# MLA's keys made with the features on the partitions, the rotated key turned once

## The chip, the cores and the metric

The kernel runs on one core of a Trainium2 chip (trn2). The metric is the device time of one execution in microseconds. The chip's engines are called here as the profile calls them: PE (TensorE, with PEld its weight loads), ACT (ScalarE), DVE (VectorE), POOL (GpSimd) and SP (SyncE).

## The reference, cut to what matters

One layer of a decoder: two attentions in parallel from one input projection, their gates, a cross-attention and an MLP, for 512 tokens of width 2048 in float32. The change concerns MLA, the second attention: 16 heads, each key of 64 features made from a normed latent of 256, and 32 rotated features that all heads share.

```python
c_q, c_kv, k_r = ...                       # columns of xn @ w_in: 512, 256, 32
q = (rmsnorm(c_q, g_q) @ w_uq).reshape(b, s, 16, 64 + 32)
q_rope = apply_rope(q[..., 64:], cos, sin)
ckv = rmsnorm(c_kv, g_kv)
k_nope = (ckv @ w_uk).reshape(b, s, 16, 64)
v = (ckv @ w_uv).reshape(b, s, 16, 64)
k_r = apply_rope(k_rope, cos, sin)         # one for all heads
sc = (q_nope . k_nope + q_rope . k_r) * 96 ** -0.5
o = softmax(causal(sc)) @ v
```

## The kernel before, in words

Every float32 operand is split into a high part (rounded by a copy on ACT) and a low part (the rest, by a subtraction on DVE); `split` does this and `mm` issues three matmuls per product: high by high, high by low, low by high. Weights come by DMA into raw tiles and are split too.

The program is one stream per engine, and its order comes from how the Python code is run. The main stream is a row of projections. `chunk` makes a projection with tokens on the partitions: for each of four token tiles `tt` it adds up the products in one PSUM tile of up to 512 columns and calls `evac`. `ft` makes a tile of one of the 32 gates (48 matmuls of 128x512), and `gate` ends it: DVE multiplies by `rbc`, ACT takes tanh, a DMA issued on ACT stores it. Between the products of a projection or gate `Side.run` lets steps of a second stream in: the attention, item by item (`attend`: scores and softmax of one item merged with the values of the item before; `flush`: the values of the last item with nothing merged), and the `post` generator of the last projection, which does the transposes. `end_post` runs the rest of a `post` at once, `drain` the rest of the post and of the attention.

PSUM has eight banks: four for `mm` tiles, three for `st` (scores and transposes) and one for the attention's output.

The MLA part: `proj_m` makes the query latent (512), the key latent (256) and the 32 features to rotate in two chunks; its `post` takes the sums of squares on ACT, rotates on POOL, then transposes the latents (three groups of four) and last works out the two roots `rq` and `rkv` in `rsqrt` (a square root on ACT, five steps on DVE). The norm's scale is thus applied later: `mla_q` and `mla_kv` evacuate with `scale=`. There are four quarters of four heads. For each `mla` runs `mla_q` (query projection, rotation, `heads_T`), some gates, `mla_kv`, some gates and a drain, while the quarter before is attended to. `mla_kv` makes 512 columns, keys of four heads and values of four heads, for one token tile at a time; the keys go with the shared rotated part, which POOL copies to each head, into rows of 96 per head, and `heads_T` turns these, four transposes a head and 16 groups of four in all. The last item of the first attention (NSA) has its values merged with the first MLA head's scores.

Of the kernel before, what the change touches and what calls it, by code (L numbers as in the profile page):

```python
# [10 lines left out]
F32R = mybir.dt.float32r  # L11
AF = mybir.ActivationFunctionType
OP = mybir.AluOpType
# [268 lines left out]
class Side:  # L282
# [20 lines left out]
            self.post = None  # L303

    def end_post(self):
        while self.post is not None:
            self.starved = False
            self.step_post()
            if self.starved and not self.step():
                raise RuntimeError("no area is free")  # L310

    def run(self, n, post):
        if post and self.post is not None:
# [17 lines left out]
class Layer:  # L331
# [619 lines left out]
    def proj_m(self, rate):  # L951
        nc = self.nc
        self.ssq = self.cp.tile([128, 8], F32, name="ssq")
        self.ssk = self.cp.tile([128, 4], F32, name="ssk")
        self.cq, self.ckv, self.cpairs = [], [], []

        def evac(c):
            def f(tt, ps):
                nc.scalar.activation(self.Rv(tt, NC_M[c]), ps, AF.Copy, scale=self.rx[:, tt:tt + 1])
            return f  # L960

        def post(c):
            for tt in range(4):
                r = self.Rv(tt, 512)
                sq = self.gst
                n = 384 if c == 0 else 128
                nc.scalar.activation(sq[:, :n], r[:, :n], AF.Square, accum_out=self.ssq[:, 4 * c + tt:4 * c + tt + 1])
                if c:
                    nc.scalar.activation(sq[:, 128:384], r[:, 128:384], AF.Square, accum_out=self.ssk[:, tt:tt + 1])
                    self.rope(r[:, 384:416].rearrange("p (n d) -> p n d", n=1), 1, 0, ROT_B, C_CB, C_SB, tt)  # L970
                    nc.gpsimd.tensor_copy(r[:, 416:448], r[:, 384:416])
            yield
            for j in range(3):
                ps = self.new_st()
                for tt in range(4):
                    nc.tensor.transpose(ps[:, tt * 128:tt * 128 + 128], self.Rv(tt, 512)[:, j * 128:j * 128 + 128],
                                        self.ident)
                f = c * 3 + j
                if f % 2 == 0:
                    self.cpairs.append(self.pairs.get())  # L980
                t, o = self.cpairs[-1], 1024 * (f % 2)
                h = HL(t[:, o:o + 512], t[:, o + 512:o + 1024])
                self.split(h, ps, self.gains[:, G_Q + f:G_Q + f + 1])
                (self.cq if f < 4 else self.ckv).append(h)
                yield
            if c:
                nc.vector.tensor_add(self.ssq[:, :4], self.ssq[:, :4], self.ssq[:, 4:])
                self.rq = self.rsqrt(self.ssq[:, :4], 4, 512, "rq")
                self.rkv = self.rsqrt(self.ssk, 4, 256, "rkv")

        for c in range(2):
            self.chunk("M", c, NC_M[c], evac(c), rate)
            self.side.post = post(c)
# [23 lines left out]
        return out  # L1017

    def mla_kv(self, q, rate):
        nc = self.nc  # L1020
        out = []
        vs = self.pairs.get()
        vv = vs[:, :2048].rearrange("p (h k d) -> p h k d", h=4, k=4)

        def evac(tt, ps):
            sc = self.rkv[:, tt:tt + 1]
            r = self.Rv(tt, 384).rearrange("p (n d) -> p n d", n=4)
            p = ps.rearrange("p (w n d) -> p w n d", w=2, n=4)
            nc.scalar.activation(r[:, :, :64], p[:, 0], AF.Copy, scale=sc)
            nc.gpsimd.tensor_copy(r[:, :, 64:], self.Rv(tt, 512)[:, None, 416:448].to_broadcast([128, 4, 32]))  # L1030
            hi, lo = vv[:, :, tt, :64], vv[:, :, tt, 64:]
            nc.scalar.activation(hi.bitcast(F32R), p[:, 1], AF.Copy, scale=sc)
            nc.vector.scalar_tensor_tensor(lo.bitcast(F32R), p[:, 1], sc, hi, op0=OP.mult, op1=OP.subtract)

        self.chunk("ukv", q, 512, evac, rate, nk=2, xs=self.ckv)
        self.side.post = self.heads_T(4, out.append)
        return out, vs

    def mla_items(self, q, qs, ks, vs):
# [10 lines left out]
    def mla(self, rate):  # L1050
        gates = deque(range(2 * KT))

        def fill(n, r=rate):
            for _ in range(min(n, len(gates))):
                self.gate(gates.popleft(), r)

        fill(T["f0"], T["rf"])
        qs = self.mla_q(0, T["rf"])
        fill(T["f1"], T["rf"])
        self.side.drain()  # L1060
        ks, vs = self.mla_kv(0, T["rf"])
        fill(T["f2"], T["rf"])
        self.side.drain()
        for q in range(4):
            self.side.add(self.attend(self.mla_items(q, qs, ks, vs)))
            if q == 3:
                break
            qs = self.mla_q(q + 1, rate)
            fill(T["f3"])
            ks, vs = self.mla_kv(q + 1, rate)  # L1070
            fill(T["f4"])
            self.side.drain()
        self.side.end_post()
        self.put(*self.cpairs, *self.R)
        self.N = []
        self.n_load = self.load_o(self.d_nsa, self.N)
        while gates:
            fill(1)
            for _ in range(2):
                if self.slots.free:  # L1080
                    next(self.n_load, None)
        self.side.drain()
        self.put(*self.X)
# [707 lines left out]
```

## Time and profile before

| what | value |
| --- | --- |
| three runs | 2912.94, 2912.91, 2905.77 us; median 2912.91 |
| the profiled execution | 2906.3 us, span 2904.5 us, granted clock 0.997 |
| busy share of the span | PE 98%, PEld 84%, DVE 65%, ACT 51%, POOL 13% |
| DMA | 446.61 MB, mean 154 GB/s |
| MLA part | about 580 to 1110 us of the span |

The span runs from the first to the last instruction; the execution is 1.8 us longer. Busy shares are means over the whole span, in which the stages differ. Rows with a time ahead show an instruction's start and length; "[2.65 <-DVE s L820]" behind a row means that its engine sat idle for 2.65 us and that DVE's instruction of line 820 ended it. Starts on one engine lie closer than the lengths say, since an instruction begins while the one before still drains.

### The profile page before, as it was taken

Reading aid. Unit: us, or ns where it says so; the run is one execution under the profiler, and the core shown is the slowest. Engines: PE = TensorE matmul, PEld = TensorE weight load, DVE = VectorE, ACT = ScalarE, POOL = GpSimd, SP = SyncE. Lnnn points to the kernel's source line nnn. Section 1 sums busy time; section 2 is a strip of 40 time slices with the busy share of each in tenths; the row PEclk is TensorE's granted clock in tenths of the full one; section 3 lists DMA queues with packets and bytes.
Section 4 is the critical chain, followed back from the end, with each engine's and each line's share of the span. In section 5 each row is a group of like instructions: output and inputs, shape, how many; then the busy total and the mean of one; then the engine's idle time right before and its main releaser. Section 6 shows DMA issues by size and latency. Waiting matters only on the chain. (4 is left out here: it accounts for less than half of the span.)

```text
span 2904.5 us, 38739 instructions
## 1 busy us (share of the span) xinstructions
PE 2854.6 (98%) x14276; PEld 2436.6 (84%) x14276; DVE 1884.5 (65%) x3225; ACT 1485.4 (51%) x2676; POOL 384.0 (13%) x637
## 2 busy tenths in 40 slices
PE   8999999999999999999999999999999999999997
PEld 8999999888888888888887778888888888888886
DVE  6346666654555555464445767677766788888887
ACT  6345555554444444333235766666666544444444
POOL 3110210002011001000100111111111111111110
PEclk9999999999999999999999999999999999999999
DMA  5322222223323345543433888888889988888895
GB/s 156 98 80 59 59 60 63 63 80 97 98 97 100 102 129 183 187 155 120 123 98 116 197 197 203 216 211 200 221 224 244 230 217 216 221 219 223 221 228 139
DMA packets 158462, 446.61 MB, mean 154 GB/s; under 512 B 16192, under 2 KB 41152, under 8 KB 158272
## 3 DMA queue, kind: packets, MB, share of 16 engines
q1 hardware_dynamic: 90560, 274.24, 29.0%
q0 software_dynamic: 36864, 134.23, 24.5%
q10 hardware_dynamic: 30848, 35.66, 3.5%
q8 instruction: 112, 1.84, 0.3%
q14 instruction: 78, 0.64, 0.1%
HBM read 406.32 MB, written 37.75 MB: 153 GB/s over the span
## 5 line engine op out<-in xcount | busy, mean ns | idle before, releaser
L371 PE MATMUL mm<-s,s 128*128 128x512 f32 (+5 forms) x2008 | 754.4, 376 | 6.3 <-ACT s L378 5.2
L373 PE MATMUL mm<-s,s 128*128 128x512 f32 (+5 forms) x2008 | 729.9, 364 | 2.8 <-DVE s L382 2.8
L372 PE MATMUL mm<-s,s 128*128 128x512 f32 (+5 forms) x2008 | 728.8, 363 | 0.2 <-DVE s L379 0.2
L379 DVE TENSOR_TENSOR s<-s,s 128x512 fp32r<-128x512 f32 (+4 forms) x558 | 366.5, 676 | 250.6 <-ACT s L378 247.2
L371 PEld LDWEIGHTS mm<-s,s 128*128 128x128 f32 x2008 | 379.8, 189 | 55.6 <-issue 5.5
L373 PEld LDWEIGHTS mm<-s,s 128*128 128x128 f32 x2008 | 378.5, 189 | 52.6 <-DVE s L382 4.8
L372 PEld LDWEIGHTS mm<-s,s 128*128 128x128 f32 x2008 | 380.3, 189 | 41.3 <-DVE s L379 1.0
L1536 PE MATMUL mm<-s,s 128*128 128x512 f32 x1024 | 399.5, 390 | 5.7 <-DVE s L1358 5.7
L1535 PE MATMUL mm<-s,s 128*128 128x512 f32 x1024 | 403.6, 394 | 0.0
L1537 PE MATMUL mm<-s,s 128*128 128x512 f32 x1024 | 399.9, 390 | 0.3 <-DVE s L1431 0.3
L378 ACT CAST s<-s 128x512 fp32r<-128x512 f32 (+4 forms) x558 | 305.5, 570 | 167.2 <-PE mm L372 54.5
L1358 DVE TENSOR_TENSOR s<-d,s 128x1024 fp32r<-128x1024 f32 x202 | 244.9, 1222 | 115.9 <-ACT s L1353 115.8
L1353 ACT CAST s<-d 128x1024 fp32r<-128x1024 f32 x202 | 209.6, 1048 | 194.7 <-DMA d<-wts 176.7
L1535 PE MATMUL st<-s,s 128*128 128x512 f32 x672 | 263.8, 393 | 0.0
L1537 PE MATMUL st<-s,s 128*128 128x512 f32 x672 | 261.9, 390 | 0.0
L1536 PE MATMUL st<-s,s 128*128 128x512 f32 x672 | 261.6, 389 | 0.0
L519 ACT ACTIVATE PP<-PP,mx 128x512 f32<-128x512 f32 (+1 forms) x208 | 116.3, 559 | 274.7 <-DVE mx L518 274.1
L1536 PEld LDWEIGHTS mm<-s,s 128*128 128x128 f32 x1024 | 192.8, 188 | 45.6 <-DVE s L1358 7.0
L1358 DVE TENSOR_TENSOR s<-s,s 128x1024 fp32r<-128x1024 f32 x150 | 181.0, 1221 | 74.8 <-ACT s L1353 74.8
L1537 PEld LDWEIGHTS mm<-s,s 128*128 128x128 f32 x1024 | 192.5, 188 | 41.8 <-DVE s L1431 1.2
L1535 PEld LDWEIGHTS mm<-s,s 128*128 128x128 f32 x1024 | 192.6, 188 | 38.4
L1353 ACT CAST s<-s 128x1024 fp32r<-128x1024 f32 x150 | 153.8, 1048 | 132.0 <-DMA s<-wts 122.9
(308 smaller groups left out, 4152.2 us busy)
## 6 DMA issues: line engine op xcount, KB each, us to landing
s<-wts SPq DMA_DIRECT2D x258, 512.0 KB, 3.7
d<-wts POOLq DMA_DIRECT2D x132, 512.0 KB, 9.8
d<-wts SPq DMA_DIRECT2D x70, 512.0 KB, 7.5
PP<-wts POOLq DMA_DIRECT2D x68, 512.0 KB, 9.5
s<-wts POOLq DMA_DIRECT2D x56, 512.0 KB, 7.3
s<-wts SPq DMA_DIRECT2D x64, 352.0 KB, 3.0
d_u<-s ACTq DMA_DIRECT2D x64, 256.0 KB, 5.6
PP<-wts SPq DMA_DIRECT2D x28, 512.0 KB, 5.4
```

The lines of the kernel that those rows point to most:

```text
L371: t.matmul(ps, a.hr, b.hr, start=first, stop=False)
L372: t.matmul(ps, a.hr, b.lr, start=False, stop=False)
L373: t.matmul(ps, a.lr, b.hr, start=False, stop=last)
L378: nc.scalar.copy(o.hr, src)
L379: nc.vector.tensor_sub(o.lr, src, o.hi)
L519: nc.scalar.activation(p, p, AF.Exp, bias=mx, scale=-1.0, accum_out=sm)
L1353: self.nc.scalar.copy(t.hr, self.raw[i])
L1358: self.nc.vector.tensor_sub(t.lr, r, t.hi)
L1535: m(ps, a.hr, b.hr, start=first, stop=False, skip_group_check=True)
L1536: m(ps, a.hr, b.lr, start=False, stop=False, skip_group_check=True)
L1537: m(ps, a.lr, b.hr, start=False, stop=last, skip_group_check=True)
```

## The change

The key latent is multiplied by its norm's scale in `proj_m` (L979) before it is turned, so that nothing behind it has to scale. `rkv` is therefore worked out ahead of the transposes. The last 96 columns of the latent's row, whose last 32 are the rotated features, are turned in a group of their own (L985) and rows 64 to 96 of the result kept as `self.kr`.

`mla_kv` makes the keys with the features on the partitions: the weights stand still, the latent's 512 tokens move, and two heads of 64 features fill the 128 partitions of one PSUM tile; there are two such tiles in a quarter. ACT copies each head's 64 rows to an SBUF tile (L1049). The values are made as before with tokens on the partitions, 256 columns for each token tile, and two token tiles lie in the two halves of one PSUM tile. ACT writes their high part (L1057), DVE the low one (L1058). A head's key is then split from its 64 rows, and the turned rotated part is copied below it (L1069, L1070); the 16 groups of head transposes for the keys are no longer there. `mla` adds `flush` behind the first `mla_q`, so the last NSA item's values run by themselves and end in the drain ahead of the first `mla_kv`.

Of the changed kernel line numbers above L307 are 3 higher, above `mla_kv` 14 (`mm` has L374 to L376 for L371 to L373, `split` L381 and L382 for L378 and L379, `gate` L1012 to L1014 for L998 to L1000).

```diff
@@ -303,11 +303,14 @@
             self.post = None
 
     def end_post(self):
+        stuck = False
         while self.post is not None:
             self.starved = False
             self.step_post()
             if self.starved and not self.step():
-                raise RuntimeError("no area is free")
+                if stuck:
+                    raise RuntimeError("no area is free")
+                stuck = True
 
     def run(self, n, post):
         if post and self.post is not None:
@@ -968,8 +971,20 @@
                 if c:
                     nc.scalar.activation(sq[:, 128:384], r[:, 128:384], AF.Square, accum_out=self.ssk[:, tt:tt + 1])
                     self.rope(r[:, 384:416].rearrange("p (n d) -> p n d", n=1), 1, 0, ROT_B, C_CB, C_SB, tt)
-                    nc.gpsimd.tensor_copy(r[:, 416:448], r[:, 384:416])
             yield
+            if c:
+                rkv = self.rsqrt(self.ssk, 4, 256, "rkv")
+                for tt in range(4):
+                    r = self.Rv(tt, 512)[:, 128:384]
+                    nc.scalar.activation(r, r, AF.Copy, scale=rkv[:, tt:tt + 1])
+                while not self.slots.free:
+                    self.side.starved = True
+                    yield
+                ps, self.kr = self.new_st(), self.slot_hl(96)
+                for tt in range(4):
+                    nc.tensor.transpose(ps[:96, tt * 128:tt * 128 + 128], self.Rv(tt, 512)[:, 320:416], self.ident)
+                self.split(self.kr[64:], ps[64:96])
+                yield
             for j in range(3):
                 ps = self.new_st()
                 for tt in range(4):
@@ -986,7 +1001,6 @@
             if c:
                 nc.vector.tensor_add(self.ssq[:, :4], self.ssq[:, :4], self.ssq[:, 4:])
                 self.rq = self.rsqrt(self.ssq[:, :4], 4, 512, "rq")
-                self.rkv = self.rsqrt(self.ssk, 4, 256, "rkv")
 
         for c in range(2):
             self.chunk("M", c, NC_M[c], evac(c), rate)
@@ -1017,23 +1031,47 @@
         return out
 
     def mla_kv(self, q, rate):
+
         nc = self.nc
         out = []
         vs = self.pairs.get()
         vv = vs[:, :2048].rearrange("p (h k d) -> p h k d", h=4, k=4)
-
-        def evac(tt, ps):
-            sc = self.rkv[:, tt:tt + 1]
-            r = self.Rv(tt, 384).rearrange("p (n d) -> p n d", n=4)
-            p = ps.rearrange("p (w n d) -> p w n d", w=2, n=4)
-            nc.scalar.activation(r[:, :, :64], p[:, 0], AF.Copy, scale=sc)
-            nc.gpsimd.tensor_copy(r[:, :, 64:], self.Rv(tt, 512)[:, None, 416:448].to_broadcast([128, 4, 32]))
+        w = self.W.get(("ukv", q, 0))
+        ps = [self.new_mm() for _ in range(4)]
+        for i in range(2):
+            for kk in range(2):
+                o = kk * 512 + i * 128
+                self.mm(ps[i], w[:, o:o + 128], self.ckv[kk], kk == 0, kk == 1)
+            self.side.run(rate / 2, True)
+        self.W.mid()
+        self.side.end_post()
+        for j in range(4):
+            nc.scalar.copy(self.Rv(j, 512)[:64], ps[j // 2][64 * (j % 2):64 * (j % 2) + 64])
+        for tt in range(4):
+            p = ps[2 + tt // 2][:, tt % 2 * 256:tt % 2 * 256 + 256]
+            for kk in range(2):
+                self.mm(p, self.ckv[kk][:, tt * 128:tt * 128 + 128], w[:, kk * 512 + 256:kk * 512 + 512],
+                        kk == 0, kk == 1)
+            p = p.rearrange("p (n d) -> p n d", n=4)
             hi, lo = vv[:, :, tt, :64], vv[:, :, tt, 64:]
-            nc.scalar.activation(hi.bitcast(F32R), p[:, 1], AF.Copy, scale=sc)
-            nc.vector.scalar_tensor_tensor(lo.bitcast(F32R), p[:, 1], sc, hi, op0=OP.mult, op1=OP.subtract)
-
-        self.chunk("ukv", q, 512, evac, rate, nk=2, xs=self.ckv)
-        self.side.post = self.heads_T(4, out.append)
+            nc.scalar.copy(hi.bitcast(F32R), p)
+            nc.vector.tensor_sub(lo.bitcast(F32R), p, hi)
+            if tt % 2:
+                self.side.run(rate / 2, True)
+
+        def post():
+            for j in range(4):
+                while not self.slots.free:
+                    self.side.starved = True
+                    yield
+                h = self.slot_hl(96)
+                self.split(h[:64], self.Rv(j, 512)[:64])
+                nc.scalar.copy(h.hr[64:], self.kr.hi[64:])
+                nc.scalar.copy(h.lr[64:], self.kr.lo[64:])
+                out.append(h)
+                yield
+
+        self.side.post = post()
         return out, vs
 
     def mla_items(self, q, qs, ks, vs):
@@ -1056,6 +1094,7 @@
 
         fill(T["f0"], T["rf"])
         qs = self.mla_q(0, T["rf"])
+        self.side.add(self.flush())
         fill(T["f1"], T["rf"])
         self.side.drain()
         ks, vs = self.mla_kv(0, T["rf"])
@@ -1071,7 +1110,7 @@
             fill(T["f4"])
             self.side.drain()
         self.side.end_post()
-        self.put(*self.cpairs, *self.R)
+        self.put(*self.cpairs, *self.R, self.kr)
         self.N = []
         self.n_load = self.load_o(self.d_nsa, self.N)
         while gates:
```

The order of instructions at the places that the prediction speaks of follows; a row is line, operation, out<-in and shape, and what it waits for. The first place is ACT after the squares of `proj_m`'s second post (L522 is the exponential of NSA's softmax, L519 before). Before:

```order
L969 ACTIVATE s_137,ssk<-s_136 128x256 [waits Activation_49]
L519 ACTIVATE PP,sm<-PP,mx 128x512 [waits DVE_49]
L519 ACTIVATE pc,csm<-pc,cmx 128x32 [waits DVE_49]
L381 ACTIVATE d_5916<-st,gains 128x512 [waits PE_49]
L519 ACTIVATE PP,sm<-PP,mx 128x384 [waits DVE_49]
L519 ACTIVATE pc,csm<-pc,cmx 128x32 [waits DVE_49]
L378 CAST s_94<-s_88 128x512
```

After:

```order
L972 ACTIVATE s_137,ssk<-s_136 128x256 [waits Activation_49]
L522 ACTIVATE PP,sm<-PP,mx 128x512 [waits DVE_49]
L522 ACTIVATE pc,csm<-pc,cmx 128x32 [waits DVE_49]
L418 ACT_TABLE_LOAD
L418 ACTIVATE rs_6289<-rs_6288 128x4 [waits DVE_49]
L979 ACTIVATE s_135<-s_135,rkv 128x256 [waits DVE_49]
L979 ACTIVATE s_135<-s_135,rkv 128x256
L979 ACTIVATE s_136<-s_136,rkv 128x256
L979 ACTIVATE s_136<-s_136,rkv 128x256 [waits Activation_49]
L381 CAST s_6303<-st 32x512 [waits PE_49]
```

The root (L418) and the four scalings of the key latent (L979) moved in behind the two exponentials, ahead of the evacuation of the first transposes.

The same place on PE, after (`d_5485` and `s_4908` are NSA's keys and queries, `s_105` a gate's weights):

```order
L374 MATMUL mm<-s_105,s_90 128x512
L375 MATMUL mm<-s_105,s_90 128x512
L376 MATMUL mm<-s_105,s_91 128x512
L985 MATMUL st<-cst,s_135 96x128 [waits PE_49,Activation_49,Pool_49]
L985 MATMUL st<-cst,s_135 96x128 [waits Activation_49,Pool_49]
L985 MATMUL st<-cst,s_136 96x128 [waits Activation_49,Pool_49] x2
L374 MATMUL st<-d_5485,s_4908 128x416 [waits DVE_49]
L375 MATMUL st<-d_5485,s_4908 128x416
```

The transposes of the rotated key stand ahead of scores and gate matmuls and wait for ACT; in before this place held the first group of L976 with no wait for ACT's scaling.

PE at the end of gate f1, ahead of the first keys. Before (`s_90` and `s_91` are the weights' parts, `d_6327` the latent):

```order
L371 MATMUL mm<-s_117,s_94 128x512
L372 MATMUL mm<-s_117,s_94 128x512
L373 MATMUL mm<-s_117,s_95 128x512
L469 MATMUL st<-cst,s_135 96x128 [waits DVE_49]
L469 MATMUL st<-cst,s_135 96x128
L469 MATMUL st<-cst,s_136 96x128 x2
L371 MATMUL mm<-s_90,d_6327 128x512
L372 MATMUL mm<-s_91,d_6327 128x512
```

After (`PP` holds the probabilities, `s_1937` to `s_1939` their turned tiles, `s_3762` NSA's values):

```order
L376 MATMUL mm<-s_117,s_95 128x512
L472 MATMUL st<-cst,s_135 96x128 [waits DVE_49]
L472 MATMUL st<-cst,s_135 96x128
L472 MATMUL st<-cst,s_136 96x128 x2
L595 MATMUL st<-cst,PP 128x128 [waits DVE_49]
L595 MATMUL st<-cst,PP 128x128 x3
L612 MATMUL o<-s_1937,s_3762 128x256 [waits Activation_49]
L613 MATMUL o<-s_1937,s_3762 128x256
L612 MATMUL o<-s_1938,s_3762 128x384 [waits Activation_49]
L613 MATMUL o<-s_1938,s_3762 128x384 [waits DVE_49]
L612 MATMUL o<-s_1939,s_3762 128x512 [waits Activation_49]
L613 MATMUL o<-s_1939,s_3762 128x512 [waits DVE_49]
L374 MATMUL mm<-d_6356,s_90 128x512
```

The last three value steps of NSA (L595, L612, L613) now stand between the gate and the first key matmul.

ACT at the second quarter's keys and values (`s_137` is the gate's tile, `s_92` weights, `s_135` and `s_136` the key rows). Before:

```order
L378 CAST s_92<-s_89 128x512 [waits DMAHW1_49,PE_49]
L653 COPY s_137<-o 64x512 [waits DMAHW6_49,PE_49]
L378 CAST s_92<-s_89 128x512
L1029 ACTIVATE s_135<-mm,rkv 128x4x64 [waits PE_49]
L1032 ACTIVATE d_7642<-mm,rkv 128x4x64
L1029 ACTIVATE s_135<-mm,rkv 128x4x64 [waits PE_49]
L1032 ACTIVATE d_7642<-mm,rkv 128x4x64
L1029 ACTIVATE s_136<-mm,rkv 128x4x64 [waits PE_49]
```

After:

```order
L1013 ACTIVATE s_137<-s_137 128x512 [waits DVE_49]
L1014 DMA d_g<-s_137 128x512 [waits Activation_49]
L381 CAST s_92<-s_89 128x512 [waits DMAHW1_49]
L381 CAST s_1937<-st 128x384 [waits PE_49]
L381 CAST s_92<-s_89 128x512
L1049 COPY s_135<-mm 64x512 [waits Pool_49] x2
L1049 COPY s_136<-mm 64x512 [waits PE_49,Pool_49]
L1049 COPY s_136<-mm 64x512 [waits Pool_49]
L1057 CAST d_7684<-mm 128x4x64 [waits PE_49]
L1057 CAST d_7684<-mm 128x4x64 [waits DVE_49,PE_49]
L1057 CAST d_7684<-mm 128x4x64 [waits PE_49]
```

The four key copies (L1049) moved ahead of the first high part of the values (L1057), where key and value parts alternated.

PE at the first quarter's values, second product of tile 0 and the first of tile 1, after:

```order
L374 MATMUL mm<-s_90,d_6356 128x256
L375 MATMUL mm<-s_91,d_6356 128x256
L376 MATMUL mm<-s_90,d_6356 128x256
L374 MATMUL mm<-s_90,d_6356 128x256 [waits DVE_49]
L375 MATMUL mm<-s_91,d_6356 128x256
L376 MATMUL mm<-s_90,d_6356 128x256
```

The matmul of the second token tile waits for DVE, whose L1058 reads the first half of the same PSUM tile; before, a token tile had a PSUM tile of its own and no such wait. The fourth token tile has the same wait, in every quarter.

## The prediction

> **What bounds the kernel now.** I read the page's totals first, then the busy time of each engine in three stretches inside the MLA part, then what the weight loads of TensorE waited for there. In the rows of stretches the columns are the stretch, its length and the busy time and instructions of PE, PEld, DVE, ACT and POOL (PE's stands twice), then the granted clock and what DMA did; in those of waits, the time, the count and the longest.
>
> ```profile
> span 2904.5 us, 38739 instructions
> PE 2854.6 (98%) x14276; PEld 2436.6 (84%) x14276; DVE 1884.5 (65%) x3225; ACT 1485.4 (51%) x2676; POOL 384.0 (13%) x637
> ```
>
> ```profile
> 700.00:800.00 100.00, 100.00 (x511) 85.15 (x510) 54.91 (x132) 46.89 (x108) 7.28 (x20) 1.00 0.31 96
> 800.00:900.00 100.00, 100.00 (x510) 84.96 (x509) 54.98 (x132) 47.07 (x108) 7.15 (x19) 1.00 0.29 97
> 900.00:1000.00 100.00, 100.00 (x501) 83.78 (x500) 54.84 (x134) 46.46 (x106) 7.78 (x20) 1.00 0.32 97
> ```
>
> ```profile
> PEld mm L371 <- DVE s L998: 0.6, 2, 0.4
> PEld mm L371 <- DVE d L1033: 0.2, 1, 0.2
> ```
>
> PE is busy for 100 us of each 100 at a clock of 1.00; ACT and DVE are half idle, POOL nearly empty. So here a removed matmul is worth its spacing in PE's queue, work moved between ACT, DVE and POOL is worth nothing while no matmul waits for it, and a new wait of PE is paid in full. What before's key and value stage makes PE wait is 0.8 us in all.
>
> **PE work removed.**
>
> ```profile
> 678.64 0.60 PE L469 MATMUL st<-cst,s 128*96 128x128 f32 x4
> 679.00 0.48 PE L371 MATMUL mm<-s,s 128*128 128x512 f32 x1
> 679.32 0.39 PE L372 MATMUL mm<-s,s 128*128 128x512 f32 x1
> 679.55 0.40 PE L373 MATMUL mm<-s,s 128*128 128x512 f32 x1
> ```
>
> ```profile
> 1195.83 0.28 PE L372 MATMUL mm<-s,s 128*128 128x256 f32 x1
> ...
> 1198.35 0.28 PE L372 MATMUL mm<-s,s 128*128 128x256 f32 x1
> 1259.71 0.39 PE L373 MATMUL mm<-s,s 128*128 128x512 f32 x1
> ...
> 1261.75 0.39 PE L373 MATMUL mm<-s,s 128*128 128x512 f32 x1
> ```
>
> The group of four head transposes and the matmul behind it take 679.32 − 678.64 = 0.68 us; a matmul of 512 alone steps by 679.55 − 679.32 = 0.23. A group costs 0.45. The sixteen groups for the keys go, one group for the rotated key comes: 15 × 0.45 = 6.75 us less. Multiplications stay the same in number of columns: per quarter before 24 of 512; after 12 of 512 and 24 of 256. The 512 ones step by 2.04/9 = 0.227, the 256 ones by 2.52/21 = 0.120 instead of 0.114: 96 × 0.006 = 0.6 more. Net −6.15. POOL's copies of the rotated key and DVE's and ACT's evacuations of the old form go or change places; none is waited for by more than the 0.8 above, which goes with them. So the most this change can give is 6.95 us.
>
> **The rotated key (L985).** It is turned from rows that L979 first multiplies by rkv, so its transposes wait for the root; in before the root came after all transposes.
>
> ```profile
> 585.51 0.60 PE L976 MATMUL st<-cst,s 128*128 128x128 f32 x4
> 586.63 0.19 ACT L519 ACTIVATION_READ_ACCUMULATOR pc<-pc,cmx 128x1 f32 x1
> 595.25 1.28 ACT L415 ACT_TABLE_LOAD   x1
> 596.54 0.21 ACT L415 ACTIVATE rs<-rs 128x4 f32<-128x4 f32 x1
> 597.39 0.17 DVE L419 SCALAR_TENSOR_TENSOR rq<-rs,rs 128x4 f32<-128x4 f32 x1
> 846.12 0.47 ACT L1029 ACTIVATE s<-mm,rkv 128x256 f32<-128x256 f32 x1 [0.42 <-PE mm L373]
> 846.49 0.47 ACT L1032 ACTIVATE d<-mm,rkv 128x256 fp32r<-128x256 f32 x1
> ```
>
> PE reaches this place at 585.51. On ACT the order puts two exponentials ahead of the root, done at 586.8. From the load of the table to the last DVE step is 597.56 − 595.25 = 2.3 us: 589.1. Four scalings of 128x256, 0.37 apart as the two at 846 are: 590.6. PE stands for 5.1 us with gate matmuls queued behind. If the root overtook nothing but the last exponential it would be 4.0; with a late row sum and the latencies, 6.5. The second pair of table loads lies on ACT alone.
> [...]
>
> **The last NSA values (flush).** They are now queued while gates of f1 run and drained before the keys; in before they lay between matmuls of the next gate.
>
> ```profile
> 841.84 0.39 PE L373 MATMUL mm<-s,s 128*128 128x512 f32 x1
> 842.27 0.69 DVE L998 TENSOR_TENSOR s<-mm,rbc 128x512 f32<-128x512 f32 x1 [2.09 <-PE mm L373]
> 842.99 0.63 ACT L999 ACTIVATE s<-s 128x512 f32<-128x512 f32 x1 [3.94 <-DVE s L998]
> 843.66 0.33 ACTq L1000 DMA_DIRECT2D d_g<-s  x1
> 844.08 0.62 ACT L378 CAST s<-s 128x512 fp32r<-128x512 f32 x1 [0.45 <-PE o L610]
> 844.60 0.58 ACT L653 COPY s<-o 64x512 f32<-64x512 f32 x1
> 844.73 0.69 DVE L379 TENSOR_TENSOR s<-s,s 128x512 fp32r<-128x512 f32 x1 [1.77 <-ACT s L378]
> 845.08 0.62 ACT L378 CAST s<-s 128x512 fp32r<-128x512 f32 x1
> 846.99 0.48 DVE L1033 SCALAR_TENSOR_TENSOR d<-mm,rkv,d 128x256 fp32r<-128x256 f32 x1 [0.24 <-ACT d L1032]
> ```
>
> In the order, the cast of the last probabilities stands on ACT behind the last gate's tanh and the issue of its DMA. Measured from that gate's last matmul (here 841.84), such a cast begins at +2.2 and DVE's low part ends at 845.42, +3.6. PE has of its own until then two groups of transposes, 1.2 us: it stands 2.4, and 0.45 at the last tile, where 0.69 of DVE exceeds two matmuls of 384. I take 2.9; 1.0 if the gate's chain runs ahead, 3.5 if DVE has a backlog.
>
> **Two halves of a bank (V).** Value tiles tt=0 and 1 share a PSUM bank, tt=2 and 3 another. In the order the first matmul of tt=1 waits for DVE's low part of tt=0 (L1058), that of tt=3 for tt=2: eight waits. DVE's part follows ACT's high part (L1057), which stands behind four key copies (L1049), which stand behind what ACT has of that moment. For the third quarter, by the rows above: from the gate's end 12 key matmuls (2.73), its last one and six of V (0.95), a value step, a score step and a transpose group (0.45 + 0.68 + 0.45) bring PE to tt=1 at +5.3. ACT's second cast ends at +3.9; an exponential comes next that needs a tile from DVE, behind DVE's 0.69 at 844.73, the output copy and another low part: 4 × 0.69 from +2.9 is +5.6. Exponential 0.7, a cast of 0.5, four copies of 0.48 (845.08 − 844.60): +8.7. High part 0.49, low part 0.5 with its start: +9.75. Wait 4.5. The last quarter has the same order: 4.5. The second has no exponential there: tanh, issue, three casts (+3.7), copies, two parts: +6.65 against PE's +3.8, 2.85. The first begins after the drain: output copy, two casts, four copies, two parts make 4.8 against 3.4, 1.4. Sum 13.3. The waits of tt=3 are 0.49 + 0.48 and two hand-overs of 0.45 together, less the 0.72 of tt=2's own second half and start: 1.2 at most, 4 × 1.2 = 4.8. Their floor: ACT idle when the V bank is full gives 1.35 and 1.2 a quarter, 10.2 in all.
> [...]
>
> **Edits at nothing.** The copies of the turned key into each head (L1069, L1070) and the key copies add twelve instructions a quarter to ACT, some 0.5 us each by the 0.48 step of a copy of 512, against eight evacuations that go: about 2 us in a quarter's 90, on an engine idle for half of them, under gates' matmuls. If that cover is gone, the first scores of the quarter are late by them, up to 2. The heads' low parts stay on DVE. DMA transfers keep number and size; the output rows of the last NSA heads are issued on ACT earlier, and nothing reads them before the end of the gates. `stuck` in `end_post` adds no instruction.
>
> **The clock.** Stalls of some microseconds can cost again.
>
> ```profile
> 167.67 0.44 PE L873 MATMUL o<-d,s 128*128 128x126 f32 x2 [2.65 <-DVE s L820]
> 168.40:171.70 3.30, 3.30 (x14) 3.30 (x13) 1.13 (x2) 0.57 (x2) 0.00 (x0) 0.50 0.28 70
> 1695.26 0.66 PE L1604 MATMUL mm<-cst,s 128*128 128x128 f32 x4 [2.10 <-DVE s L1558]
> 1695.30:1698.70 3.40, 3.40 (x17) 2.90 (x18) 1.68 (x2) 2.88 (x4) 0.88 (x1) 1.00 1.02 178
> 2876.04 0.79 PE L1536 MATMUL mm<-s,s 128*128 128x512 f32 x1 [4.38 <-DVE s L1358]
> 2876.10:2881.80 5.70, 5.70 (x22) 5.11 (x23) 3.84 (x12) 3.35 (x6) 0.00 (x0) 0.50 0.12 33
> ```
>
> 2.65 idle microseconds were followed by at least 3.3 at half clock, 4.38 by at least 5.7, 2.10 by none. Half of 3.4 lost is 1.7 per stall: the rotated key and three of the V waits reach 2.65, 4 × 1.7 = 6.8. Bounds 0 (none falls) and 20 (six stalls at 3.4 each).
> [...]
>
> **Sum.** −6.15 − 0.8 + 5.1 + 2.9 + 13.3 + 4.8 + 6.8 = +26, on the profiled execution's 2906.3: 2932. The runs are 2905.77, 2912.91 and 2912.94, so this execution is 6.6 under their median; against their middle I say 2935.
>
> **Rivals.**
> 1. The waits stay at their floors: 10.2 at the V banks, 1.0 at the drain, the clock untouched. For it speaks that ACT is half idle; against it the order, which puts copies ahead of the high parts. −6.95 + 5.1 + 1.0 + 10.2 = +9.4: 2916.
> 2. Not slower: the half-bank waits are covered, because the merged attention matmuls in `side.run` fall between the halves or the copies run far ahead of PE. Then −6.95 + 5.1 + 2.9 + 1.7 = +2.8: 2909, no change. It decides when the eight waits together are under 8.7 − 2.8 = 5.9 us, 1.5 a quarter. Against it: the order puts nothing between the six matmuls of tt=0 and the first of tt=1. Faster by more than 0.3% would need the other stalls gone too, and 6.95 falls short of 8.7 even so.
> 3. The clock answers as at 2876, and at six stalls: 20 instead of 6.8, 2906.3 + 39 = 2946.
>
> **Chances and range.** 0.3%, 8.7 us, is about what a measurement of this kernel can tell from no change. Forecast 0.58 (2922 to 2942), rival 1 0.20 (lies on the mark: 0.12 slower, 0.08 no change), rival 2 0.13 (0.09 no change, 0.04 faster), rival 3 0.09. Slower 0.79, same 0.17, faster 0.04. The range leaves out most of rival 2 and the far end of rival 3: 2912 to 2952, the top being rival 3 with the upper prices of the rotated key and the drain.
>
> **What would show it.** L985 with an idle time of about 5 us before it, ended by ACT's L979. L374 of 128x256 waiting for DVE's L1058 eight times, 1.2 to 4.5 us each. A wait at L613 for DVE before the first keys. Granted clock under 1.00 in the microseconds behind those. 64 fewer transposes at the heads. I am wrong if L1058 ends no idle time of PE (rival 2), or if L1049 runs well before the V banks fill (rival 1).

## The result and the profile after

The changed kernel takes 2939.43 us in the median (2937.59 to 2944.99, four runs) against 2909.38 for the kernel before (2905.77 to 2912.94, four runs): a ratio of 1.011, 95% interval 1.0097 to 1.0122. It is slower, by about 30 us. The profiled execution is 2937.9 us with a span of 2936.1, 31.6 more than before. Its totals, and PE's waits in the MLA part (line waited at, what ended the wait, total, count, longest):

```profile
span 2936.1 us, 38743 instructions
PE 2862.4 (97%) x14264; PEld 2443.7 (83%) x14264; DVE 1887.0 (64%) x3226; ACT 1513.4 (52%) x2715; POOL 379.5 (13%) x617
```

```profile
PE mm L374 <- DVE d L1058: 18.5, 8, 4.8
PE st L985 <- issue: 4.1, 1, 4.1
PE o L612 <- ACT s L381: 2.6, 1, 2.6
PE o L613 <- DVE s L382: 0.7, 2, 0.4
```

Eight waits for the low part of a value tile, one at the rotated key, two in the drain: 25.5 us, where before had 1.0 (the second wait at L613 in this list, 0.44 us, stands behind the last gate in both kernels). One of the three stretches that were full before, and then the MLA part as a whole, in before and in the change, from ACT's first square of the key latent (L969, now L972) to DVE's multiplication of the last gate:

```profile
900.00:1000.00 100.00, 94.33 (x470) 80.50 (x469) 51.36 (x125) 48.73 (x108) 6.92 (x16) 0.95 0.30 91
```

```profile
583.23:1097.55 514.32, 513.22 (x2578) 431.73 (x2577) 280.46 (x697) 243.75 (x569) 34.63 (x91) 1.00 0.32 102
583.50:1129.36 545.86, 520.32 (x2566) 438.74 (x2565) 281.98 (x699) 270.20 (x608) 30.52 (x71) 0.97 0.31 96
```

PE is no longer busy throughout, and the granted clock, third from the end, is 0.95 in the one and 0.97 in the other. The matmuls that waited longest, and one of the four second waits at the value tiles (all 0.92 us), with the idle time in brackets:

```profile
590.04 1.66 PE L985 MATMUL st<-cst,s 128*96 128x128 f32 x4 [4.10 <-issue]
681.93 0.50 PE L612 MATMUL o<-s,s 128*128 128x512 f32 x1 [2.61 <-ACT s L381]
689.25 0.39 PE L374 MATMUL mm<-s,d 128*128 128x256 f32 x1 [2.64 <-DVE d L1058]
691.87 0.39 PE L374 MATMUL mm<-s,d 128*128 128x256 f32 x1 [0.92 <-DVE d L1058]
761.78 0.39 PE L374 MATMUL mm<-s,d 128*128 128x256 f32 x1 [2.70 <-DVE d L1058]
867.76 0.58 PE L374 MATMUL mm<-s,d 128*128 128x256 f32 x1 [4.75 <-DVE d L1058]
976.06 0.58 PE L374 MATMUL mm<-s,d 128*128 128x256 f32 x1 [4.75 <-DVE d L1058]
```

And the stretches at half clock, with PE's busy time and the clock; three begin within one of these waits, that of 762.70 begins 0.92 us behind the end of the 2.70:

```profile
588.62:595.45 6.83, 5.38 (x15) 3.82 (x16) 2.87 (x12) 5.32 (x12) 0.00 (x0) 0.50 0.00 0
762.70:769.53 6.83, 5.91 (x24) 5.23 (x23) 2.74 (x6) 3.18 (x7) 0.00 (x0) 0.50 0.01 2
865.10:875.34 10.24, 6.66 (x24) 5.95 (x25) 3.02 (x8) 4.84 (x11) 0.00 (x0) 0.50 0.04 13
974.32:984.56 10.24, 7.58 (x27) 6.70 (x28) 3.18 (x7) 4.62 (x11) 0.00 (x0) 0.50 0.01 2
```

PE did 25.53 us of its work at half clock. A matmul of 512 columns stepped by 0.43 us there and one of 256 by 0.21, against 0.23 and 0.12 at full clock, so half of it, 12.8 us, is put down to the clock, as an estimate. The MLA part is 31.5 us longer: PE's idle time there rose by 24.4, from 1.1 to 25.5, the clock cost 12.8, and the rest of PE's busy time fell by 5.7.

Where the time is lost can be read off the gates: DVE's multiplication that ends the fourth, the eighth and the last gate, before and after.

```profile
646.70 0.67 DVE L998 TENSOR_TENSOR s<-mm,rbc 128x512 f32<-128x512 f32 x1
729.59 0.68 DVE L998 TENSOR_TENSOR s<-mm,rbc 128x512 f32<-128x512 f32 x1
1097.55 0.69 DVE L998 TENSOR_TENSOR s<-mm,rbc 128x512 f32<-128x512 f32 x1 [4.32 <-PE mm L373]
```

```profile
652.53 0.67 DVE L1012 TENSOR_TENSOR s<-mm,rbc 128x512 f32<-128x512 f32 x1
741.29 0.69 DVE L1012 TENSOR_TENSOR s<-mm,rbc 128x512 f32<-128x512 f32 x1 [1.41 <-PE mm L376]
1129.36 0.69 DVE L1012 TENSOR_TENSOR s<-mm,rbc 128x512 f32<-128x512 f32 x1 [4.32 <-PE mm L376]
```

5.8 us are lost once the rotated key's place is passed, 11.7 by the end of the first quarter's keys, 31.8 at the last gate, and the span ends 31.6 later: the loss lies in the MLA part alone (0.3 us of each shift were there at its start, 583.50 against 583.23).

### The profile page after: what moved, and what is told of

It is laid out like the page before. It is cut to its first block, busy times and chain, and to the rows that moved or that the text cites. A ratio compares the mean times of both kernels' runs of the same rounds, so it can differ in the third digit from the quotient of the medians.

```text
span 2936.1 us, 38743 instructions
## 1 busy us (share of the span) xinstructions
PE 2862.4 (97%) x14264; PEld 2443.7 (83%) x14264; DVE 1887.0 (64%) x3226; ACT 1513.4 (52%) x2715; POOL 379.5 (13%) x617
## 3 DMA queue, kind: packets, MB, share of 16 engines
q8 instruction: 112, 1.84, 0.3%
## 5 line engine op out<-in xcount | busy, mean ns | idle before, releaser
L374 PE MATMUL mm<-s,s 128*128 128x512 f32 (+5 forms) x2008 | 755.3, 376 | 6.3 <-ACT s L381 5.2
L376 PE MATMUL mm<-s,s 128*128 128x512 f32 (+5 forms) x2008 | 731.4, 364 | 2.8 <-DVE s L385 2.6
L382 DVE TENSOR_TENSOR s<-s,s 128x512 fp32r<-128x512 f32 (+5 forms) x574 | 379.5, 681 | 258.8 <-ACT s L381 254.1
L374 PEld LDWEIGHTS mm<-s,s 128*128 128x128 f32 x2008 | 380.8, 190 | 56.3 <-issue 5.7
L376 PEld LDWEIGHTS mm<-s,s 128*128 128x128 f32 x2008 | 379.7, 189 | 53.5 <-DVE s L385 4.9
L381 ACT CAST s<-s 128x512 fp32r<-128x512 f32 (+5 forms) x574 | 314.7, 571 | 167.8 <-PE mm L375 52.9
L522 ACT ACTIVATE PP<-PP,mx 128x512 f32<-128x512 f32 (+1 forms) x208 | 116.3, 559 | 271.7 <-DVE mx L521 271.0
```

Of the source, the lines that this page charges most:

```text
L374: t.matmul(ps, a.hr, b.hr, start=first, stop=False)
L376: t.matmul(ps, a.lr, b.hr, start=False, stop=last)
L381: nc.scalar.copy(o.hr, src)
L382: nc.vector.tensor_sub(o.lr, src, o.hi)
L522: nc.scalar.activation(p, p, AF.Exp, bias=mx, scale=-1.0, accum_out=sm)
```

## The experiments

A number for the span or for a wait is from the profiled execution of that kernel. The program ahead of the MLA part is the same in all kernels, yet the traces enter that part at different times:

```profile
583.23 0.41 ACT L969 ACTIVATE s<-s 128x256 f32<-128x256 f32 x1
580.65 0.41 ACT L972 ACTIVATE s<-s 128x256 f32<-128x256 f32 x1
585.55 0.41 ACT L972 ACTIVATE s<-s 128x256 f32<-128x256 f32 x1
```

These are the first squares of before, of the kernel with more steps in f1 and of the one with the chain taken apart. So two kernels are compared here by the length from that square to the last gate's multiplication, 514.32 us in before:

| kernel | ratio of the times to before | MLA part against before, us |
| --- | --- | --- |
| the change | 1.011 | +31.5 |
| four banks | 1.003 | +10.2 |
| value tiles 0 and 2 ahead | 1.0017 | +8.2 |
| key copies behind the values | one run | +19.2 |
| rotated key's transposes later | 1.0109 | +32.0 |
| rotated key's chain taken apart | 1.0112 | +28.6 |
| more steps in f1 | 1.0118 | +33.3 |
| before, 12 groups left out | 0.9975 | -5.4 |
| four repairs together | 1.001 | +2.1 |
| two repairs more | 0.9988 | -3.2 |
| the same, scalings on POOL | 0.9999 | -1.9 |

Single repairs first.

**Four banks for four value tiles.**

```diff
-        ps = [self.new_mm() for _ in range(4)]
+        ps = [self.new_mm() for _ in range(2)]
...
-            p = ps[2 + tt // 2][:, tt % 2 * 256:tt % 2 * 256 + 256]
+            p = self.new_mm()[:, :256]
```

> The changed kernel, with each of the four value tiles of a quarter in a PSUM bank of its own (the third and fourth take over the banks of the keys). Theory (the stalls): the eight waits for DVE's low part, 18.5 us, go; instead the third tile waits for ACT's key copies, about 2 us in the third and fourth quarter and nothing in the first two, and none of these stalls is long enough to halve the clock. The profiled execution falls by about 25 us from 2937.9 to 2913, and the granted clock rises from 0.991 to about 0.996. Rival (the wait only changes its name): ACT's copies hold PE as long as before, the waits for them come to 15 to 18 us and the time stays within 5 us of 2938. Second rival (the loss lies in the 256-column matmuls and the new order, not in waits): the time stays though the waits are gone.

2917.58 us, ratio 1.003 (1.0018 to 1.0041). Of the value tiles' waits these are left:

```profile
756.14 0.39 PE L374 MATMUL mm<-s,d 128*128 128x256 f32 x1 [0.23 <-ACT s L1049]
854.85 0.39 PE L374 MATMUL mm<-s,d 128*128 128x256 f32 x1 [1.97 <-ACT s L1049]
957.86 0.39 PE L374 MATMUL mm<-s,d 128*128 128x256 f32 x1 [1.96 <-ACT s L1049]
959.07 0.39 PE L374 MATMUL mm<-s,d 128*128 128x256 f32 x1 [0.23 <-ACT s L1049]
```

18.5 us of waits became 4.4, now for the key copies in whose banks the third and fourth tiles lie, and the span fell from 2936.1 to 2915.5. The expectation's 2913 was 4 too low for the execution (2917.24); both rivals fall. That no stall would halve the clock was wrong: it was at half for 3.4 us behind L985, behind L612 and behind the 1.97 at 854.85. Two thirds of the loss are the shared bank and the clock behind its waits.

**Value tiles 0 and 2 ahead of the keys.** The bank is shared as in the change, but 12 key matmuls stand between its halves on PE, and the high parts of tiles 0 and 2 stand ahead of the key copies on ACT.

```diff
+        value(0)
+        value(2)
         for i in range(2):
...
-        for tt in range(4):
+        for tt in (1, 3):
+            value(tt)
+            self.side.run(rate / 2, True)
```

> The changed kernel, still with two value tiles in a bank, but with tiles 0 and 2 made ahead of the keys and tiles 1 and 3 behind them, so that 12 key matmuls (2.7 us) stand between the two halves of a bank. Theory: the waits for L1058 fall from 18.5 us to some 3.6 (1.8 each in the third and fourth quarter, none in the others), the half clock in those places goes, and the time falls by about 25 to 2912. Rival (ACT is late anyway, by whatever the gate and the softmax left on it): the waits for ACT or DVE in the key and value stages still come to over 10 us in all, and the time falls by under 12.

2913.79, ratio 1.0017 (1.0008 to 1.0026). No matmul waits for a value tile any more; what waits is the next gate, whose PSUM tile is the first key tile's:

```profile
859.90 0.50 PE L374 MATMUL mm<-s,s 128*128 128x512 f32 x1 [1.22 <-ACT s L1062]
960.68 0.50 PE L374 MATMUL mm<-s,s 128*128 128x512 f32 x1 [1.34 <-ACT s L1062]
```

L1062 is the key copy. So it was not the sharing as such but what comes between the two halves. On PE that is now 2.7 us of key matmuls; on ACT the high parts of the third quarter run at 853.75, ahead of an exponential (857.48) and the key copies (858.67). This run doesn't say which of the two is worth how much.

**Key copies behind the values.**

```diff
-        for j in range(4):
-            nc.scalar.copy(self.Rv(j, 512)[:64], ps[j // 2][64 * (j % 2):64 * (j % 2) + 64])
         for tt in range(4):
...
+        for j in range(4):
+            nc.scalar.copy(self.Rv(j, 512)[:64], ps[j // 2][64 * (j % 2):64 * (j % 2) + 64])
```

> The changed kernel, with the four key copies on ACT behind the values instead of ahead of them. Theory (the copies are 4 x 0.48 us of each first wait): the first waits for L1058 fall by 1.9 us each, to about 0.7, 0.8, 2.9 and 2.9, the second ones stay at 0.9; the gate behind now waits for the key copies, 1 to 1.5 us a quarter. Rival (the first waits are set by the softmax and the casts ahead of the copies): they stay within 0.5 of 2.6, 2.7, 4.75 and 4.75.

One run: 2924.3 us. First and second wait of the first quarter and first wait of the last two (L1056 is the low part here):

```profile
687.12 0.38 PE L374 MATMUL mm<-s,d 128*128 128x256 f32 x1 [0.92 <-DVE d L1056]
689.74 0.39 PE L374 MATMUL mm<-s,d 128*128 128x256 f32 x1 [0.92 <-DVE d L1056]
859.87 0.39 PE L374 MATMUL mm<-s,d 128*128 128x256 f32 x1 [2.64 <-DVE d L1056]
963.13 0.38 PE L374 MATMUL mm<-s,d 128*128 128x256 f32 x1 [2.65 <-DVE d L1056]
```

The first waits fell from 2.64, 2.70, 4.75 and 4.75 to 0.92, 0.92, 2.64 and 2.65, by 1.7 to 2.1 each: the four copies are that part, and what stands ahead of the high part on ACT in the last two quarters, an exponential and a cast, is the other 1.7. The eight waits together fell from 18.5 to 10.8. 0.92 is what a hand-over from PE to ACT to DVE and back costs here with nothing ahead of it. The wait expected at the gate did not come; the one new wait, 0.38 us, stands at a query projection and is for DVE's multiplication of a gate.

**The rotated key's transposes later.**

```diff
                     nc.scalar.activation(r, r, AF.Copy, scale=rkv[:, tt:tt + 1])
+                for _ in range(4):
+                    yield
```

> The changed kernel, with four more steps of the gates' products between the scaling of the key latent and the transposes of the rotated key. Theory: the stall of 4.1 us before L985 goes, and with it the half clock behind it (1.7 us): 2937.9 falls by about 6 to 2932; the clock in the stretch 580 to 620 is 1.00. Rival: the transposes are late for what needs them, and the wait comes back at the first gate or at the first keys: no change.

2941.48, ratio 1.0109 (1.0092 to 1.0126): no gain. The wait at the transposes is gone and stands elsewhere:

```profile
596.00 0.55 PE L595 MATMUL st<-cst,PP 128*128 128x128 f32 x3 [3.47 <-DVE s L382]
```

ACT's rows there tell why (those of two exponentials between 593.51 and 594.42 are left out):

```profile
588.16 1.28 ACT L418 ACT_TABLE_LOAD   x1
589.45 0.20 ACT L418 ACTIVATE rs<-rs 128x4 f32<-128x4 f32 x1
590.50 1.71 ACT L979 ACTIVATE s<-s,rkv 128x256 f32<-128x256 f32 x4 [0.84 <-DVE rkv L422]
592.21 1.28 ACT L522 ACT_TABLE_LOAD   x1
594.42 0.60 ACT L381 CAST s<-s 128x512 fp32r<-128x512 f32 x1
```

From 588.2 to 594.4 ACT makes no cast, behind 3 us of squares, so weights and probabilities come late. The rival is right: the transposes were only the first of several to wait for the same chain.

**The rotated key's chain taken apart.** A group of query transposes first, both roots on one table load three steps later, the scalings four steps later, the transposes two steps later.

```diff
+                if c and j == 1:
+                    for _ in range(3): yield
+                    ...  # rkv and rq
+                    for _ in range(4): yield
+                    ...  # four scalings on ACT
+                    for _ in range(2): yield
+                    ...  # transposes and split of self.kr
```

> The changed kernel, with the rotated key's chain taken apart: first one group of query transposes, three steps of the gates later both roots on one table load (rq here too), four steps later the scaling, two steps later the transposes of the rotated key. In the order ACT then loads the table behind the same exponentials as before the change. Theory now (what costs is that ACT holds the softmax of NSA for about 6 us while squares, table load, root and scalings stand in a row; moving only the transposes moved the wait to L595): no wait over 1 us at this place, the first four gates end as in before within 0.6 us, and 2937.9 falls by 3 to 7, to about 2933. Rival (any second table load or scaling on ACT must be paid by PE): a wait of 3 us or more appears at another line near 590 to 615.

2940.08, ratio 1.0112 (1.0098 to 1.0125). The whole time shows no gain, but its interval is 0.3% wide, 8 us; in the trace the MLA part is 3.0 us shorter than the change's, the low end of the expected 3 to 7. The table load is hidden: the first gate ends 17.71 us behind the first square, where before takes 19.60. But behind the four scalings, 1.7 us of ACT in a row, the scores' PSUM tile comes free late (the kernel with the scalings on POOL, further down, shows that they are only part of it):

```profile
611.09 0.44 PE L374 MATMUL st<-d,s 96*128 96x384 f32 x1 [2.29 <-DVE mx L521]
```

That wait with half clock behind it costs 5.1 us up to the second gate. The expected "no wait over 1 us" is missed, and the rival's 3 us is not reached.

**More steps in gate f1.**

```diff
-        fill(T["f1"], T["rf"])
+        fill(T["f1"], 1.7)
```

> The changed kernel, with more attention steps let in between the products of gate f1 (1.7 for 1.2), so that the last values of NSA end among that gate's matmuls and not in the drain. Theory: the two waits at L612 and L613, 2.8 us, go, and 0.2 us of restart each; 2937.9 falls to about 2934.7. Rival: the steps still wait for the same casts and the time stays at 2938.

2943.6, ratio 1.0118 (1.0103 to 1.0133): no gain. The waits at L612 and L613 are gone, and the first wait for a value tile grew from 2.64 to 4.46, with half clock behind it:

```profile
684.21 0.58 PE L374 MATMUL mm<-s,d 128*128 128x256 f32 x1 [4.46 <-DVE d L1058]
```

PE reaches that place 6.9 us earlier, DVE's low part comes only 5.0 earlier, because ACT's tanh, weight casts, copies and high part stand in a row behind the gate. Neither the expected gain nor the rival's reason is what happened: the drain's wait had been taken off the next one.

**Transposes alone.** The kernel before, with 12 of the 16 groups of key transposes left out: three heads of four get the first one's keys.

```diff
-        self.side.post = self.heads_T(4, out.append)
+                if ps is None:
+                    ps = self.new_st()
+                    ...  # the four transposes of the first head
+                h = self.slot_hl(96)
+                self.split(h, ps[:96, :])
```

> The kernel before, with only the first head's four transposes made in each quarter; the other three heads' keys are split from the same PSUM tile, so 12 groups of transposes are left out and three heads of four get the first one's keys. Theory: 12 x 0.45 = 5.4 us less, 2906.3 to 2901. Rival (transposes are hidden, since the casts behind them pace the heads): no change.

2901.26, ratio 0.9975 (0.9966 to 0.9985). The gates move up by 1.4 us in each quarter, and the MLA part is 5.4 us shorter, 0.45 a group, as read from the trace of before.

**Repairs together.** Value tiles 0 and 2 ahead, chain taken apart, 1.7 steps in f1, and every second key copy on DVE:

```diff
-            nc.scalar.copy(self.Rv(j, 512)[:64], ps[j // 2][64 * (j % 2):64 * (j % 2) + 64])
+            f = nc.vector.tensor_copy if j % 2 else nc.scalar.copy
+            f(self.Rv(j, 512)[:64], ps[j // 2][64 * (j % 2):64 * (j % 2) + 64])
```

> The changed kernel with value tiles 0 and 2 ahead of the keys, the spread chain of the rotated key, 1.7 steps in gate f1, and the second and fourth key copy on DVE. Theory (the change is worth its 15 groups of transposes, 6.95 us at most, once the stalls are gone): waits in the MLA part of 1 to 3 us in all, no half clock, and 2900 to 2903 against 2906.3 of before, a ratio of 0.998 to 0.999. Rival (waits move on, as with the two single repairs): 4 us or more of new waits at the casts and at the gates behind the keys, and a time no better than 2906.

2911.09, ratio 1.001 (1.0001 to 1.0019). PE still waits 2.29 us behind the scalings, 1.09 at the first value tile and 1.67 each for the key copies in the last two quarters: the rival's outcome. Two steps more were tried, first each pair of keys copied right behind its matmuls and the scalings one to a step:

```diff
+        self.side.end_post()
         for i in range(2):
...
+            for j in (2 * i, 2 * i + 1):
+                ...  # copy on ACT or DVE
             self.side.run(rate / 2, True)
...
                         nc.scalar.activation(r, r, AF.Copy, scale=rkv[:, tt:tt + 1])
+                        yield
```

> As the version with four repairs (value tiles 0 and 2 ahead of the keys, spread chain, 1.7 steps in f1, key copies on ACT and DVE by turns), with two more: each pair of keys is copied right behind its matmuls, ahead of the attention steps that are let in there, and the four scalings of the key latent go one to a step of the gates. Theory (in the version with four repairs, 906.3 + 2000 of span, what is left is one wait of 2.3 us behind the scalings with its half clock, 5 us together, and two waits of 1.7 us for the key copies): these go, and the span falls from 2906.3 to about 2899, a ratio of 0.998 against the kernel before (0.995 to 1.000). Rival (ACT's load in those places is what counts, and a wait of 2 us or more appears behind whatever stands there): 2904 or more.

2905.08 against 2908.14, ratio 0.9988 (0.998 to 0.9997), span 2901.2, where 2899 was expected. What PE still waits for in the MLA part:

```profile
609.83 0.44 PE L595 MATMUL st<-cst,PP 128*128 128x128 f32 x2 [0.71 <-DVE s L382]
679.86 0.38 PE L374 MATMUL mm<-s,d 128*128 128x256 f32 x1 [1.09 <-DVE d L1055]
848.11 0.50 PE L374 MATMUL mm<-s,s 128*128 128x512 f32 x1 [0.24 <-DVE s L1066]
948.26 0.50 PE L374 MATMUL mm<-s,s 128*128 128x512 f32 x1 [0.24 <-DVE s L1066]
```

No stretch of the MLA part has a clock under 1.00, and it is 3.2 us shorter than in the kernel before. Then the four scalings on POOL in a row:

```diff
-                        nc.scalar.activation(r, r, AF.Copy, scale=rkv[:, tt:tt + 1])
+                        nc.gpsimd.tensor_scalar(r, r, rkv[:, tt:tt + 1], None, op0=OP.mult)
```

> As the kernel with two more repairs, with the four scalings of the key latent on POOL in a row instead of on ACT one to a step. Theory: POOL is idle there, the time is as that kernel's or up to 1.5 us better. Rival (the rotation's or the key rows' waits for POOL grow, or POOL is far slower at 128x256): a wait of PE or ACT for POOL of over 2 us.

2907.07, ratio 0.9999 (0.999 to 1.0008): not faster than before. A wait of 1.61 us at the same scores is back; no wait of over 2 us for POOL. With the scalings on ACT in a row it had been 2.29, so their time on ACT was about 0.7 of that wait. The rest goes when the scalings are spread over the gates' steps; that it is the steps themselves and what they let in between is argued, not shown.

## Why the prediction was right, point by point

The time (2939) lies 4 us above the 2935 forecast, and the forecast's mechanism is the one that ran.

- PE work removed: 0.45 us a group, confirmed by leaving groups out of the kernel before. In the change PE's work fell by 5.7, with the 12.8 of the clock taken off, where 6.15 was forecast.
- The rotated key: 5.1 us forecast, 4.10 idle measured. The profile names "issue" and not L979; the matmul waits for several semaphores, and in three other kernels a second wait there, of 0.16 us, does name L979. That only the transposes pay for that stretch of ACT was too narrow: with these moved away, the first probabilities' transposes waited for casts that stood behind the same stretch.
- The drain: 2.9 forecast, 2.61 and 0.22 measured. That it is a loss by itself was wrong: taken away alone, it came back at the value tiles.
- The value tiles: 18.1 forecast, 18.5 measured. The first waits were put at 1.4, 2.85, 4.5 and 4.5 and were 2.64, 2.70, 4.75 and 4.75, the second ones at 1.2 and were 0.92. The floor of 2.55 a quarter was too high as well: in the first two quarters with the copies behind the values it is 1.84. The first quarter was under-sized because DVE's output addition and the issue of its DMA stand ahead of the weight casts on ACT, which the sum left out:

```profile
684.90 1.14 ACT L381 CAST s<-s 128x512 fp32r<-128x512 f32 x2 [1.13 <-DVE s L657]
```

- The clock: 6.8 forecast, at 1.7 for each of four stalls; 12.8 by the estimate above, half of the 25.53 us of work measured in the four stretches. The number of stalls was right. This is the mis-sized term: the clock was at half for 6.8 or 10.2 us a stall, not for the 3.4 that before has behind its wait of 2.65 (168.34 to 171.75). With it the terms (24.4 of idle time, 12.8 of clock, 5.7 less work) make the 31.5 of the MLA part.
- Rival 2 needed the halves' waits under 1.5 us a quarter. They were 3.56 to 5.67. The tiles made ahead of the keys show what it would have taken: key matmuls between the halves, with the high part ahead of the copies on ACT.

This case's trace has the wait between the halves in all eight places, at 0.92 us and more. Whether a kernel needs it isn't shown: none here leaves it out where two value tiles share a bank.

## What to carry to other kernels

Where the matmul engine is full, as in before (100 us of each 100 from 700 to 1000), an operation removed there was worth its spacing here (0.45 us a group of transposes, some 6 in all), and every new hand-over must be checked for what stands between producer and consumer on each queue. Two tiles in one PSUM bank were a hand-over here, 0.92 us at the least. Put other matmuls between them and the read of the first half early in its queue: in the kernel with that repair alone no matmul waited for a value tile, and in the change what stood ahead in ACT's queue was paid (1.7 to 2.1 us a first wait for the key copies, 1.7 more in the last two quarters for an exponential and a cast). A repair that removes one wait proves little until the next wait on the same chain is looked at: three of six single repairs gained nothing in the whole time here, and only together, with the copies and scalings spread out, did they end below the kernel before, by 0.1%, and with the scalings on POOL not clearly. And compare stages of two traces from a common start: the parts ahead differ by up to 4.9 us here without any change in them, as much as some repairs are worth.

## What the runs showed of the hardware

The same stall did not always cost the same. Behind the wait of 4.10 us at L985 the clock was at half for 6.8 us in the change and in the kernel with tiles ahead, and for 3.4 in those with four banks, with the copies behind the values and with more steps in f1. From the first square to the first gate it is 24.97 and 25.56 us in the first two and 24.38, 24.31 and 24.35 in the others, against 19.60 in before. The wait of 2.61 at L612 was followed by a clock of 1.00 in the change, and by 0.50 in the kernel with tiles ahead of the keys. The first three rows are of the change, the last two of the other:

```profile
585.21:588.62 3.41, 0.73 (x4) 0.25 (x2) 0.17 (x1) 3.36 (x12) 0.36 (x2) 1.00 0.00 0
677.38:680.79 3.41, 1.94 (x15) 1.47 (x13) 1.90 (x4) 1.18 (x3) 0.00 (x0) 1.00 0.25 88
680.79:684.20 3.41, 2.05 (x8) 1.47 (x9) 1.09 (x2) 1.27 (x3) 0.00 (x0) 1.00 0.22 82
679.67:683.08 3.41, 1.31 (x11) 0.99 (x9) 1.32 (x3) 1.34 (x3) 0.00 (x0) 1.00 0.09 34
683.08:686.49 3.41, 2.90 (x10) 2.37 (x11) 1.39 (x2) 1.03 (x2) 0.00 (x0) 0.50 0.23 82
```

What differs is how the stall lies to the steps in which the clock changes. In the traces of before and of the change the falls and rises of the clock lie whole multiples of 3.413 us apart: the change's falls at 588.62, 762.70, 865.10 and 974.32 are 51, 30 and 32 such steps from one to the next, before's first two, at 168.34 and 2875.11, are 793. With the two traces cut into these steps, from the first record of the clock on, at 11 us, there are eleven at a clock of 1.00 in which PE was idle for 2.08 us or more, and half clock followed each; in all others at 1.00 PE was idle for 1.71 or less, and it followed none. In the change the edge at 680.79 parts the wait of 2.61 into two steps, with 1.47 and 1.36 us of idle time (0.22 of it from the wait behind); in the other kernel 2.10 of it fall into one. The first row is the step of the stall at L985, 2.68 of it idle.

That an equal stall is followed by half clock in one run and not in another fits these steps; that they decide it is the author's reading, and no run tried it alone. So a stall of some 2 us or more had a price of its own here, from 0 us (the 2.61 at L612 in the change) to 3.8 (the 4.75 at 976.06, an estimate: half of the 7.58 of work at half clock from 974.32 on), which no average of one trace gives.
